# Moving the memory gate into the attention loop, the combination by one step, and two weight splits out of their queue, in an encoder block on one core

## The chip, the cores and the metric

The kernel runs on one core of a Trainium2 chip. A core has a matrix engine (TensorE, PE in the profile; PEld is its loading of weights), a vector engine (VectorE, DVE), an activation engine (ScalarE, ACT), a general engine (GpSimd, POOL) and a queue engine that only starts transfers (SyncE, SP). Each takes its instructions in order. Transfers between the large memory (HBM) and the on-chip memory (SBUF) are DMAs. The accumulators of PE lie in PSUM banks. The metric is device time in microseconds (us) for one execution, less is better.

## The reference

One encoder block on a sequence of 1024 tokens with 1024 channels. Three mixers run on the same normalised input: a windowed attention in three dilation groups (a), a grouped-query attention (b), and an attention into a fixed memory of 256 rows (m). Each is multiplied by a SiLU gate and projected, the three are merged by sigmoid gates, and one output projection follows.

```
h = rms_norm(x, g_pre);  a_qkv, bq, bk, bv, mq, ga, gb, gm, mg = split(h @ w_in)
# a: three groups (window, dilation), combined by the softmax of their log-denominators
wts = softmax(stack(lses));  oa = sum_g wts[g] * outs[g]
# b: rms-normed, axially rotated queries and keys, 8 query heads over 2 key heads
p = softmax(qc . kb * HEAD_DIM ** -0.5);  ob = p @ vb
# m: queries into the memory
pm = softmax(mq . km * M_HEAD_DIM ** -0.5);  om = pm @ vm
ya = (oa * silu(ga)) @ w_br_a;  yb = (ob * silu(gb)) @ w_br_b;  ym = (om * silu(gm)) @ w_br_m
gates = sigmoid(mg + b_merge)
merged = gates[0] * ya + gates[1] * yb + gates[2] * ym
x = x + rms_norm(merged @ w_out, g_post)
```

Everything is float32. The kernel keeps that by splitting an operand into a high and a low part and taking three products (high by high, high by low, low by high).

## The kernel before

The stages follow each other on PE, whose order is written out by hand: projections and the memory attention (to about 200 us), the grouped-query attention (to 461), the products of the windowed attention's values (a Strassen scheme, to 587), the products of its queries and keys (`pair_product`, L1312, 587 to 1079), the windowed attention itself woven with the first 16 of 24 branch units (1079 to 1298), the last 8 units (`y_part`, L2015), and the output projection (L2097). PE is never given work out of this order, so an operand that is late stops it. From the values stage on the order of DVE, ACT, POOL and SP is by hand too.

**Grouped-query attention** (`b_att`). A loop over n does, each for an own lag, `row_max` (n below 128), `scores` ten steps and more later, `pv` and `final`. Between them it yields the time in which another stream of projections is fed to PE. POOL adds up the exponentials of a block (L788), ACT and DVE split the sum (`lh`, `ll`), and `final` multiplies it by a column of ones (L125). `token_block` uses the tiles `tx0`, `tx1`, `tb0` to `tb3` at n = 18 to 90 and not after.

**Third values stage**. 28 steps n (7 products of 4 blocks), each of 12 matmuls (L1273). A dictionary `SIDE` gives for each n the instructions that are issued to the other engines after that step's matmuls: sums (`v3_sum`) on DVE, splits (`v3_split`: high part on ACT, low part on DVE, L105 and L106) of the products' operands S1 to S4, `operand` (the gate of b), `k_load` and the like for the next stage, and, before the change, `memory_operand`: two loads (`od[2, k]` and `g2d[2, k]`) into the two tiles `tab`, 0.5 × a × gate on DVE, a store. The same two tiles are then loaded with a rotation table (`tabA`) which is multiplied by `rb`; the pair products' evacuations read it.

**Windowed attention.** 12 items (4 pairs of heads by 3 groups), each of 8 steps T. `plan` puts the work of a step into a list, `weave` mixes it on PE with the units of `add_y`. After the third group of a pair `combine` gives 12 functions: `fetch` the denominators, `shares`, `weights`, `put` (a store), two loads, two `weigh` (POOL), and so on. `combining(T)` issues the next as long as T equals its entry in `STEP_T`. `tokens(T)` issues what belongs to single items, at the last item the four loads of `rows`, which `shares_3` transposes on PE (L1911).

**Branch units.** Unit m multiplies a column block of the three projections by the gated mixer output. `y_load(m)` loads weights (SP), `y_split(m)` splits them: high part on ACT (L1345), low part on the engine given, DVE or POOL (L1346), into a `wh` tile unless another is given. `th_load` loads the merge gate, and `y_evac` (L1363, L1364) adds the unit up on DVE. Unit m of the weave leaves such calls in the list `pend`, from which the weave takes one at a time. Behind the weave come the rest of `pend`, then `third(1)` (three DVE instructions, L1957 to L1959, the last of the combination of pair 3, which read and free the bank `W3B[2, 1]`), `dl_high(3, hi)` (ACT, L1851), `dl_low`, and the units 16 to 18 in three parts:

```python
for ks in (range(2), range(2, 3)):
    for m in range(16, 19):
        y_part(m, ks)
```

then their fourth blocks of k and the units 19 to 23, each with `y_evac(m - 1)`, at m = 16 and 17 `y_split(m + 3)`.

Of the kernel before, what the change touches and what calls it, by code (L numbers as in the profile page):

```python
# [8 lines left out]
F32 = mybir.dt.float32  # L9
R = mybir.dt.float32r  # L10
AF = mybir.ActivationFunctionType
OP = mybir.AluOpType
# [3 lines left out]
S = 1024  # L16
NT = 8
P = 128
# [32 lines left out]
def block(ctx: ExitStack, tc: tile.TileContext, x, xT, memT, cst, msk, bcst, tabA, gpost,  # L51
          wu, wv, wb, wmem, wbr, wout, out):
    nc = tc.nc
# [120 lines left out]
    pend = []  # L174
# [525 lines left out]
    with tc.tile_pool(name="ba", bufs=1, reuse_waits="tile") as ba:  # L700
# [34 lines left out]
        def token_block(k):  # L735
# [13 lines left out]

            return [sub(0, b12, b11), sub(2, b22, b12), sub(1, b22, T[0]), sub(3, b21, T[1])]  # L750

        def b_att():
            st = {}
            blocks = []
# [66 lines left out]
            for n in range(128 + LAG_F + 8):  # L821
                if n < 128:
                    i, x = divmod(n, 8)
                    row_max(i, x)
                    if n == 1:
                        b_const()
                    if n in (18, 42, 66, 90):
                        blocks += token_block((n - 18) // 24)
                    if blocks and x in (1, 3) and n % 24 != 19:
                        with tc.issue_after(fp["last"].ins):  # L830
                            blocks.pop(0)()
                    yield 216
                    if i % 2 and i < 15 and x == 4:
                        q_prep((i + 1) // 2)
                        yield 436
                else:
                    yield END_PAD
                if n % 8 == LAG_S % 8 and 0 <= n - LAG_S < 128:
                    shift((n - LAG_S) // 8)
                    yield 109  # L840
                m = n - LAG_T
                if m < 0:
                    yield START_PAD + 1000 * (n < 3)
                elif m < 128:
                    scores(*divmod(m, 8))
                    yield 432
                m = n - LAG_P
                if 0 <= m < 128 and m % 8 == 7:
                    pv(m // 8)
                    yield 8 * 432  # L850
                m = n - LAG_F
                if m >= 0 and m % 8 == 7 and m < 128:
                    final(m // 8)
                    yield 432
# [127 lines left out]
    def operand(r, stage):  # L982
# [10 lines left out]
            V.tensor_tensor(ot, ot, rt, op=OP.mult)  # L993
        else:
            nc.sync.dma_start(od[1, k, :, t], OT.pop(r)[0])

    def memory_operand(k, stage):

        if stage == 0:
            nc.sync.dma_start(tab[0], od[2, k])  # L1000
            nc.sync.dma_start(tab[1], g2d[2, k])
        else:
            V.scalar_tensor_tensor(tab[0], tab[0], 0.5, tab[1], op0=OP.mult, op1=OP.mult)
            nc.sync.dma_start(od[2, k], tab[0])

    turn = [0]

# [203 lines left out]
    for n in range(28):  # L1211
# [34 lines left out]
        if k == 3:  # L1246
# [2 lines left out]
    SIDE = {2: [lambda: v3_sum("S2", "A22", "S3", OP.subtract, v3.tile([P, 1024], F32, name="xS2"))],  # L1249
            4: [lambda: v3_split("S2")], 5: [lambda: kt_split("T3", 0)], 6: [lambda: kt_split("T3", 1)],   # L1250
            7: [lambda: operand(7, 1), lambda: operand(7, 2)], 8: [lambda: v3_split("S3")],
            10: [lambda: v3_sum("S4", "A12", "S2", OP.subtract)], 12: [lambda: v3_split("S4")],
            13: [lambda: k_load(0, 0)], 14: [lambda: v3_sum("S1", "A11", "S2", OP.add)], 16: [lambda: v3_split("S1")],
            18: [lambda: k_load(0, 1)], 20: [lambda: v3_split("A22"), lambda: k_load(1, 0)], 22: [lambda: k_load(1, 1)],
            23: [lambda: k_sum(0, 1)], 24: [lambda: k_own(0)], 25: [lambda: [k_sum(0, j) for j in (2, 3)]],
            26: [lambda: k_block(0, "S2")], 27: [lambda: k_block(0, "S1"), lambda: k_block(0, "S3"), lambda: k_sum(0, 4)]}
    for j in range(4):
        for z in range(2):
            SIDE.setdefault(2 + 5 * j + 4 * z, []).append(lambda j=j, z=z: memory_operand(j, z))
    SIDE[22].append(lambda: [nc.sync.dma_start(tab[j], tabA[:, j]) for j in range(2)])  # L1260
    for j in range(2):
        SIDE[26 + j].append(lambda j=j: V.tensor_tensor(tab[1 - j], tab[1 - j], rb, op=OP.mult))
    for n in range(28):
        i, k = divmod(n, 4)
        an, bn = PRODUCTS[i]
# [205 lines left out]
    with ExitStack():  # L1471
# [218 lines left out]
        def plan(it, pre, nxt):  # L1690
# [7 lines left out]
            def tokens(T):  # L1698
# [11 lines left out]
                if n == 11:  # L1710
                    if T == 6:
                        DL["g"] = cb.tile([P, S], F32, name="wgt", bufs=2)
                        nc.sync.dma_start(DL["g"], g2d[0, 3])
                    if T == 5:
                        for j in range(4):
                            nc.scalar.dma_start(rows[16 * j:16 * j + 16],
                                              std[3, j % 2, j // 2].rearrange("s (t a) -> (s t) a", t=NT))

            def ready():
# [104 lines left out]
                    lambda: load(2), load_gate, lambda: weigh(2), gate, store]  # L1824

        todo = []
        STEP_T = (4, 7, 0, 0, 1, 5, 5, 7, 0, 3, 4, 6)
        seq = [(p_, g) for p_ in range(4) for g in range(3)]
        items = [item(*x) for x in seq] + [None]

# [25 lines left out]
        def add_y(m):  # L1856
            n, i, f = steps[m]

            def gen(_):
# [2 lines left out]
                    pend.append(lambda: y_split(m + 1, G))  # L1862
                if m == 15:
                    pend.append(lambda: y_load(18))
                pend.append(lambda: th_load(m + 1))
                for t in half:
                    ps_ = psd()
# [106 lines left out]
        weave(16, every(), FIRST_PAD + 12 * NT * (SOFT + 100.0) + 4 * LAST_PAD + 10500.0)  # L1974
        while pend:
            pend.pop(0)()
        third(1)
        dl_high(3, hi)
        dl_low(3, lo)
        y_split(17)  # L1980
        dl_low(3, hi)
        y_split(18, V, qk.tile([P, S], R, name="aq", bufs=2))
        y_load(19)
        out_pool()
        for nm in ("B11", "B21"):
            for k in range(4):
# [341 lines left out]
```

## Time and profile before

| | us |
|---|---|
| three runs | 1434.96, 1439.09, 1443.1 (median 1439.09) |
| profiled execution | 1439.34, its span 1437.5, mean granted clock 0.988 |
| PE busy | 1395.1 (97%) |
| DVE, ACT, POOL busy | 1023.4, 659.1, 573.1 |

The span is the time between the first and the last instruction that the profile shows; 1.84 us of the execution lie around it. An engine is idle where its next instruction waits for another engine, or for a DMA; the profile names the one that came last. The granted clock is the share of full speed that PE was given in a stretch.

### The profile page before, as it was taken

Reading aid. Unit: us, or ns where it says so; the run is one execution under the profiler, and the core shown is the slowest. Engines: PE = TensorE matmul, PEld = TensorE weight load, DVE = VectorE, ACT = ScalarE, POOL = GpSimd, SP = SyncE. Lnnn points to the kernel's source line nnn. Section 1 sums busy time; section 2 is a strip of 40 time slices with the busy share of each in tenths; the row PEclk is TensorE's granted clock in tenths of the full one; section 3 lists DMA queues with packets and bytes.
Section 4 is the critical chain, followed back from the end, with each engine's and each line's share of the span. In section 5 each row is a group of like instructions: output and inputs, shape, how many; then the busy total and the mean of one; then the engine's idle time right before and its main releaser. Section 6 shows DMA issues by size and latency. Waiting matters only on the chain.

```text
span 1437.5 us, 21813 instructions
## 1 busy us (share of the span) xinstructions
PE 1395.1 (97%) x7775; PEld 1113.6 (77%) x7775; DVE 1023.4 (71%) x1824; ACT 659.1 (46%) x1384; POOL 573.1 (40%) x440
## 2 busy tenths in 40 slices
PE   8999999999999998899999999999999999998997
PEld 7799986666666888788888888888887777776886
DVE  7768578776763786766777776677776556667877
ACT  6544356665645443233333333333346664652332
POOL 1416703767665000244555554455541253360003
PEclk9999999999999999999999999999999999998999
DMA  6356432222111887624332333333365677755455
GB/s 239 96 170 230 167 121 87 97 77 89 63 52 42 284 258 253 208 81 127 102 101 99 108 117 118 103 117 103 118 199 175 211 184 210 226 171 183 141 204 176
DMA packets 120284, 212.29 MB, mean 148 GB/s; under 512 B 32400, under 2 KB 60912, under 8 KB 120176
## 3 DMA queue, kind: packets, MB, share of 16 engines
q1 hardware_dynamic: 110384, 196.88, 42.7%
q10 hardware_dynamic: 9792, 14.03, 2.7%
q8 instruction: 61, 1.00, 0.3%
q14 instruction: 47, 0.39, 0.1%
HBM read 144.48 MB, written 66.38 MB: 147 GB/s over the span
## 4 chain that ended last, share of the span: by engine, by line
PE 52%; DMA 4%; DVE 3%; SPq 1%; POOL 1%; issue 1%; ACT 0%; ACTq 0%; DVEq 0%; POOLq 0%
PE s L1312 33%; PE d L1872 4%; PE s L2097 4%; PE sc L2015 3%; PE s L1572 2%; PE d L2097 2%; PE tr L1644 1%; DMA tab<-g2d 1%; DMA avs<-vdr 1%; PE tr L1611 1%; DMA od<-tab 1%; PE tr L1620 1%; PE tr L1637 1%; DVE acc L1364 0%; DMA tab<-in_tabA 0%
## 5 line engine op out<-in xcount | busy, mean ns | idle before, releaser
L788 POOL TENSOR_TENSOR bl<-bl,bp 128x512 f32<-128x512 f32 x96 | 130.5, 1360 | 54.3 <-ACT bp L784 48.9
L1312 PE MATMUL s<-hh,vS 128*128 128x512 f32 x400 | 133.4, 395 | 0.0
L1312 PE MATMUL s<-vA,vS 128*128 128x512 f32 x450 | 106.6, 390 | 0.0
L106 DVE TENSOR_TENSOR vS<-vot,vS 128x512 fp32r<-128x512 f32 x75 | 86.4, 1152 | 19.9 <-ACT vS L105 19.9
L1585 ACT ACTIVATE pra<-pra,sts 128x192 f32<-128x192 f32 (+2 forms) x176 | 75.4, 430 | 53.2 <-DVE sts L1584 48.7
L1312 PEld LDWEIGHTS s<-vA,vS 128*128 128x128 f32 x450 | 84.5, 188 | 18.3
L784 ACT ACTIVATE bp<-s 128x512 f32<-128x512 f32 x128 | 75.8, 595 | 43.4 <-PE s L782 42.5
L764 DVE TENSOR_REDUCE bn<-tr 128x1 f32<-128x512 f32 x128 | 84.9, 683 | 12.1 <-PE tr L763 11.0
L143 PE MATMUL d<-hh,wh 128*128 128x512 f32 x224 | 89.9, 401 | 2.4 <-DVE fth L216 2.4
L147 PE MATMUL d<-hh,wl 128*128 128x512 f32 x224 | 90.1, 402 | 0.0
L145 PE MATMUL d<-hl,wh 128*128 128x512 f32 x224 | 89.6, 400 | 0.0
L1312 PEld LDWEIGHTS s<-hh,vS 128*128 128x128 f32 x400 | 75.3, 188 | 17.7
L1312 PE MATMUL s<-hh,wl 128*128 128x512 f32 x200 | 79.7, 399 | 2.6 <-DVE wl L106 2.6
L1312 PE MATMUL s<-hh,wh 128*128 128x512 f32 x200 | 79.5, 398 | 0.3 <-ACT wh L105 0.3
L1312 PE MATMUL s<-hl,vS 128*128 128x512 f32 x200 | 79.1, 395 | 0.0
L1312 PE MATMUL s<-hl,wh 128*128 128x512 f32 x200 | 78.7, 394 | 0.0
L1053 POOL TENSOR_TENSOR vot<-wr 128x512 f32<-128x512 f32 x13 | 22.2, 1709 | 127.0 <-DMA vA<-in_wu 127.0
L1623 DVE COPY app<-tr 128x384 f32<-128x384 f32 (+1 forms) x64 | 38.8, 606 | 43.9 <-PE tr L1611 27.6
L1316 ACT ACTIVATE vv<-s 128x512 f32<-128x512 f32 x50 | 29.9, 598 | 85.1 <-PE s L1312 58.6
L797 PE MATMUL ov<-bp,VS 128*64 128x512 f32 x256 | 58.5, 598 | 0.0
L1053 POOL TENSOR_TENSOR vot<-vot,vA 128x512 f32<-128x512 f32 x12 | 19.3, 1609 | 91.5 <-DVE vS L106 91.5
L143 PEld LDWEIGHTS d<-hh,wh 128*128 128x128 f32 x224 | 42.6, 190 | 16.3 <-issue 5.5
(619 smaller groups left out, 4097.6 us busy)
## 6 DMA issues: line engine op xcount, KB each, us to landing
wr<-in_wu SPq DMA_DIRECT2D x40, 512.0 KB
vA<-in_wu SPq DMA_DIRECT2D x24, 512.0 KB
qkd<-ko SPq DMA_DIRECT2D x96, 128.0 KB
wl<-thd SPq DMA_DIRECT2D x24, 512.0 KB
wos<-os SPq DMA_DIRECT2D x12, 512.0 KB
wr<-in_wbr SPq DMA_DIRECT2D x24, 256.0 KB
aq<-qkd SPq DMA_DIRECT2D x12, 512.0 KB
ak<-qkd SPq DMA_DIRECT2D x12, 512.0 KB
```

What stands on the lines that cost most here:

```text
L106: V.tensor_tensor(dst_l, src, dst_h.bitcast(F32), op=OP.subtract)
L143: PE.matmul(dst, wh[:, k, :], hh[k][:, t], start=k == 0, stop=False)
L145: PE.matmul(dst, wh[:, k, :], hl[k][:, t], start=False, stop=False)
L147: PE.matmul(dst, wl[:, k, :], hh[k][:, t], start=False, stop=k == 7)
L764: fp["last"] = V.tensor_reduce(st[i]["n"][:, j, c:c + 1], s, axis=AX.X, op=OP.min)
L784: A.activation(pp, s, AF.Exp, scale=-1.0)
L788: G.tensor_tensor(lsum[i % 2], lsum[i % 2], pp, op=OP.add)
L797: PE.matmul(o[e * 64:e * 64 + 64], VS[:, kt, kv], d.pop(kt), start=kt < 2, stop=kt >= NT - 2)
L1312: PE.matmul(BANK[n, c], a, b, start=k == 0 and q == 0 and not more, stop=k == 3 and q == 2, skip_group_check=c in "XW")
L1585: A.activation(src, src, AF.Exp, scale=-1.0, bias=bias, accum_out=sts[:, h, 1, T:T + 1])
L1872: PE.matmul(ps_, a, b, start=k == 0 and q == 0, stop=k == 3 and q == 2)
L2097: PE.matmul(dst[:, e[0]:e[1]], a, b, start=k == 0 and q == 0, stop=k == 3 and q == 2)
```

## The change

- `memory_operand` leaves the third values stage. In its place `memory_load` and `memory_gate` do the same in `b_att`: the loads at n = 112, 116, 130, 132, in halves of 128 × 512, into the tiles `tx` and `tb`; the gates at n = 128, 129, 137, 139, two DVE instructions and two stores each.
- In `SIDE` the loads of `tabA` move from n = 22 to n = 9, the products by `rb` from n = 26 and 27 to n = 13 and 17.
- `STEP_T` moves most functions of a combination by one step.
- The loads of `rows` go from ACT's queue at T = 5 to SP's, two at T = 2 and two at T = 6.
- `y_split(17)` is left in `pend` at unit 15, with its low part on DVE, into a tile named `ak` (in which the windowed attention keeps its keys). `y_split(18)` (into `aq`, the queries' tile) and `y_load(19)` are issued before `third(1)` instead of at the end.

```diff
@@ -749,6 +749,24 @@
 
             return [sub(0, b12, b11), sub(2, b22, b12), sub(1, b22, T[0]), sub(3, b21, T[1])]
 
+        MT = {}
+
+        def memory_load(k):
+            if k % 2 == 0:
+                t = [ba.tile([P, S], F32, name=f"tx{j}", bufs=1) for j in range(2)]
+                MT[k] = [[x[:, h] for h in half] for x in t]
+            else:
+                t = [ba.tile([P, 512], F32, name=f"tb{j}", bufs=1) for j in range(4)]
+                MT[k] = [t[0:2], t[2:4]]
+            for src, dst in zip((od, g2d), MT[k]):
+                for j in range(2):
+                    nc.sync.dma_start(dst[j], src[2, k, :, half[j]])
+
+        def memory_gate(k):
+            for j, (o, g) in enumerate(zip(*MT.pop(k))):
+                V.scalar_tensor_tensor(o, o, 0.5, g, op0=OP.mult, op1=OP.mult)
+                nc.sync.dma_start(od[2, k, :, half[j]], o)
+
         def b_att():
             st = {}
             blocks = []
@@ -838,6 +856,10 @@
                 if n % 8 == LAG_S % 8 and 0 <= n - LAG_S < 128:
                     shift((n - LAG_S) // 8)
                     yield 109
+                if n in (112, 116, 130, 132):
+                    memory_load((112, 116, 130, 132).index(n))
+                if n in (128, 129, 137, 139):
+                    memory_gate((128, 129, 137, 139).index(n))
                 m = n - LAG_T
                 if m < 0:
                     yield START_PAD + 1000 * (n < 3)
@@ -993,15 +1015,6 @@
             V.tensor_tensor(ot, ot, rt, op=OP.mult)
         else:
             nc.sync.dma_start(od[1, k, :, t], OT.pop(r)[0])
-
-    def memory_operand(k, stage):
-
-        if stage == 0:
-            nc.sync.dma_start(tab[0], od[2, k])
-            nc.sync.dma_start(tab[1], g2d[2, k])
-        else:
-            V.scalar_tensor_tensor(tab[0], tab[0], 0.5, tab[1], op0=OP.mult, op1=OP.mult)
-            nc.sync.dma_start(od[2, k], tab[0])
 
     turn = [0]
 
@@ -1249,17 +1262,14 @@
     SIDE = {2: [lambda: v3_sum("S2", "A22", "S3", OP.subtract, v3.tile([P, 1024], F32, name="xS2"))],
             4: [lambda: v3_split("S2")], 5: [lambda: kt_split("T3", 0)], 6: [lambda: kt_split("T3", 1)], 
             7: [lambda: operand(7, 1), lambda: operand(7, 2)], 8: [lambda: v3_split("S3")],
+            9: [lambda: [nc.sync.dma_start(tab[j], tabA[:, j]) for j in range(2)]],
+            13: [lambda: k_load(0, 0), lambda: V.tensor_tensor(tab[1], tab[1], rb, op=OP.mult)],
+            17: [lambda: V.tensor_tensor(tab[0], tab[0], rb, op=OP.mult)],
             10: [lambda: v3_sum("S4", "A12", "S2", OP.subtract)], 12: [lambda: v3_split("S4")],
-            13: [lambda: k_load(0, 0)], 14: [lambda: v3_sum("S1", "A11", "S2", OP.add)], 16: [lambda: v3_split("S1")],
+            14: [lambda: v3_sum("S1", "A11", "S2", OP.add)], 16: [lambda: v3_split("S1")],
             18: [lambda: k_load(0, 1)], 20: [lambda: v3_split("A22"), lambda: k_load(1, 0)], 22: [lambda: k_load(1, 1)],
             23: [lambda: k_sum(0, 1)], 24: [lambda: k_own(0)], 25: [lambda: [k_sum(0, j) for j in (2, 3)]],
             26: [lambda: k_block(0, "S2")], 27: [lambda: k_block(0, "S1"), lambda: k_block(0, "S3"), lambda: k_sum(0, 4)]}
-    for j in range(4):
-        for z in range(2):
-            SIDE.setdefault(2 + 5 * j + 4 * z, []).append(lambda j=j, z=z: memory_operand(j, z))
-    SIDE[22].append(lambda: [nc.sync.dma_start(tab[j], tabA[:, j]) for j in range(2)])
-    for j in range(2):
-        SIDE[26 + j].append(lambda j=j: V.tensor_tensor(tab[1 - j], tab[1 - j], rb, op=OP.mult))
     for n in range(28):
         i, k = divmod(n, 4)
         an, bn = PRODUCTS[i]
@@ -1711,9 +1721,9 @@
                     if T == 6:
                         DL["g"] = cb.tile([P, S], F32, name="wgt", bufs=2)
                         nc.sync.dma_start(DL["g"], g2d[0, 3])
-                    if T == 5:
-                        for j in range(4):
-                            nc.scalar.dma_start(rows[16 * j:16 * j + 16],
+                    if T in (2, 6):
+                        for j in (0, 1) if T == 2 else (2, 3):
+                            nc.sync.dma_start(rows[16 * j:16 * j + 16],
                                               std[3, j % 2, j // 2].rearrange("s (t a) -> (s t) a", t=NT))
 
             def ready():
@@ -1824,7 +1834,7 @@
                     lambda: load(2), load_gate, lambda: weigh(2), gate, store]
 
         todo = []
-        STEP_T = (4, 7, 0, 0, 1, 5, 5, 7, 0, 3, 4, 6)
+        STEP_T = (4, 0, 1, 1, 2, 6, 6, 7, 2, 3, 4, 6)
         seq = [(p_, g) for p_ in range(4) for g in range(3)]
         items = [item(*x) for x in seq] + [None]
 
@@ -1862,6 +1872,7 @@
                     pend.append(lambda: y_split(m + 1, G))
                 if m == 15:
                     pend.append(lambda: y_load(18))
+                    pend.append(lambda: y_split(17, V, qk.tile([P, S], R, name="ak", bufs=2)))
                 pend.append(lambda: th_load(m + 1))
                 for t in half:
                     ps_ = psd()
@@ -1974,13 +1985,12 @@
         weave(16, every(), FIRST_PAD + 12 * NT * (SOFT + 100.0) + 4 * LAST_PAD + 10500.0)
         while pend:
             pend.pop(0)()
+        y_split(18, V, qk.tile([P, S], R, name="aq", bufs=2))
+        y_load(19)
         third(1)
         dl_high(3, hi)
         dl_low(3, lo)
-        y_split(17)
         dl_low(3, hi)
-        y_split(18, V, qk.tile([P, S], R, name="aq", bufs=2))
-        y_load(19)
         out_pool()
         for nm in ("B11", "B21"):
             for k in range(4):
```

## The prediction

> **What bounds the kernel now.** I read the page's head first, then the waits of TensorE, then stretches of the span with the granted clock, last the chain of what ended last and the instructions around each wait. The head:
>
> ```profile
> span 1437.5 us, 21813 instructions
> PE 1395.1 (97%) x7775; PEld 1113.6 (77%) x7775; DVE 1023.4 (71%) x1824; ACT 659.1 (46%) x1384; POOL 573.1 (40%) x440
> ```
>
> TensorE (PE) is busy for 97% of the span and the diff removes no matmul. So the kernel gets shorter only where PE stands still or runs below full clock. The waits of PE (total, times, longest, in us):
>
> ```profile
> PE s L1273 <- ACT wh L105: 5.8, 1, 5.8
> PE sc L2015 <- ACT wh L1345: 4.5, 1, 4.5
> PE s L1312 <- ACT vv L1316: 2.7, 1, 2.7
> PE s L1312 <- DVE wl L106: 2.6, 1, 2.6
> ...
> PE s L1572 <- DVE sts L1584: 2.0, 3, 1.6
> PE sc L2015 <- DVE acc L1364: 1.9, 1, 1.9
> ```
>
> These six rows, 19.5 us, lie in three places: the third values stage (L1273, and the start of the pair products at L1312), one step of the windowed attention (L1572), and the output units after it (L2015). Each is paid for twice. Two stretches (length; busy us of PE, PEld, DVE, ACT, POOL; granted clock; DMA share; GB/s), each holding one of those short gaps:
>
> ```profile
> 1200.00:1210.00 10.00, 8.45 (x66) 6.68 (x64) 6.27 (x27) 4.56 (x20) 0.00 (x0) 0.83 0.71 214
> 1320.00:1330.00 10.00, 8.13 (x29) 6.23 (x28) 9.90 (x13) 2.71 (x5) 0.00 (x0) 0.83 0.64 220
> ```
>
> If the clock only takes full and half speed, 0.83 over 10 us is 3.4 us at half, which costs PE 1.7 us of work. So a gap of 1.6 or 1.9 us costs about 1.7 us beyond itself.
>
> **A, the third values stage.** The four memory operands (load, gate, store) leave it, and the table's loads and products (`tab`, `rb`) move from its end (n=22, 26, 27) to n=9, 13, 17. The chain (start, us) enters the pair products through the table's load:
>
> ```profile
> 588.39 5.56 DMA tab<-in_tabA
> ...
> 601.42 478.12 PE s L1312 x2076
> ```
>
> The instructions (start, us, engine, operation; in brackets the idle time before and its releaser), and one grouped row (busy us, mean ns):
>
> ```profile
> 556.42 1.23 DVE L1003 SCALAR_TENSOR_TENSOR tab<-tab,tab 128x1024 f32<-128x1024 f32 x1 [7.13 <-DMA tab<-g2d]
> 560.47 1.04 ACT L105 ACTIVATE wh<-vS 128x1024 fp32r<-128x1024 f32 x1
> 538.30 0.28 PE L1273 MATMUL s<-wh,hh 128*128 128x256 f32 x1
> 555.45 0.28 PE L1273 MATMUL s<-wl,ak 128*128 128x256 f32 x1
> 561.56 0.80 PE L1273 MATMUL s<-wh,vA 128*128 128x256 f32 x2 [5.83 <-ACT wh L105]
> L1262 DVE TENSOR_TENSOR tab<-tab,rb 128x1024 f32<-128x1024 f32 x2 | 4.2, 2118 | 0.5 <-DMA tab<-in_tabA 0.5
> ```
>
> The gate of the second operand stands in VectorE's (DVE's) queue ahead of work for the next product; it waits 7.13 us for its load, what is behind it reaches ScalarE (ACT) late, and PE stops for 5.83. At the stage's end the two table products (2.12 each) wait for their load and stand ahead of the evacuations that PE needs: the waits of 2.6 and 2.7. Without waits the stage would be 28 steps of 12 matmuls, 336. The start at 555.45 is the 144th, so one is (555.45 − 538.30)/143 = 0.12, and they take 40.3; then 24 pair-product matmuls, to be taken at 0.23 (the spacing in the rows of part C), are 5.5. That ends at 584.1, where the row stands at 601.42: 17.3 us, gaps and half clock together. What becomes late next is the product's operand S3 itself: what stands behind the gate on DVE moves up, but its own loads are no earlier. I leave 0.8 for that: **16.5**, between 12 (a 2 us wait with its 1.7, and small ones) and 17.3.
>
> **B, the combination a step later.** The fetch of `cpt` stays at T=4; the shares move from T=7 to T=0 of the next item; weights, put, the first two loads and their weighings move one step later, `load_gate` two; the third load and weighing, the gate and the store stay.
>
> ```profile
> 1198.35 0.17 DVE L1783 TENSOR_TENSOR cmn<-cpt 128x16 f32<-128x16 f32 x1 [2.80 <-DMA cpt<-std]
> 1202.85 0.37 PE L1572 MATMUL s<-ak,aq 64*128 64x128 f32 x1 [1.55 <-DVE sts L1584]
> ```
>
> DVE waits 2.80 us for `cpt` in one of the three combinations, and PE then 1.55 for DVE. Those 1.55 and the 1.7 of clock go when the load has one step more: the windowed attention runs from 1079.54 (where the chain's row above ends) to 1298.03 (part C), 12 items of 8 steps, so a step is about 2.2. That is 3.3 at most, 0 if the wait returns; I take **3.0**. Three instructions of 0.2 on DVE, one small one on ACT and the DMAs of `put` and the loads keep their number and lie under PE's matmuls; POOL's weighings, and the splits behind them, are the last rival below. On SP the third load (T=7) now comes one step after the first weighing (T=6), which frees its buffer, instead of two: if that holds SP for a microsecond, it is the loads of the values (`avs`, `avp`) behind it that pay, and these are why I don't take the full 3.3.
>
> **C, the output units.** `y_split(17)` leaves ACT's queue behind `dl_high(3, hi)` and goes into unit 15, in a tile that is free; `y_split(18)` and `y_load(19)` go ahead of `third(1)`.
>
> ```profile
> 1302.07 0.68 DVE L1957 TENSOR_TENSOR og<-tr,og 128x512 f32<-128x512 f32 x1
> 1304.24 0.63 ACT L1851 ACTIVATE hh<-og 128x512 fp32r<-128x512 f32 x1 [2.76 <-DVE og L1959]
> 1304.78 0.61 ACT L1345 ACTIVATE wh<-wr 128x512 fp32r<-128x512 f32 x1
> 1318.81 0.63 ACT L1345 ACTIVATE wh<-wr 128x512 fp32r<-128x512 f32 x1 [5.54 <-PE sc L2015]
> 1298.03 0.40 PE L2015 MATMUL sc<-hh,wh 128*128 128x512 f32 x1
> 1310.37 0.39 PE L2015 MATMUL sc<-hh,aq 128*128 128x512 f32 x1
> 1313.12 0.39 PE L2015 MATMUL sc<-hh,wh 128*128 128x512 f32 x1
> 1323.31 0.52 PE L2015 MATMUL sc<-hh,wh 128*128 128x512 f32 x1 [1.87 <-DVE acc L1364]
> ```
>
> The split of unit 17 starts at 1304.78, right behind `dl_high(3, hi)`, which needs `third(1)` on DVE; PE waits 4.48 for it. Later `y_split(19)` waits 5.54 for a `wh` buffer that units 16 and 17 hold; with `ak` used there is one more. The evacuation of unit 16 stands behind it on DVE, and PE waits 1.87. Units 16 to 18 are 72 matmuls (3 units, 4 blocks of k, 2 halves, 3 products); 12 of them lie between 1310.37 and 1313.12, so one is 0.229 and all are 16.5. From 1298.03 they end at 1314.5 where unit 19 starts at 1323.31. Two splits (0.69 each) now stand ahead of `third(1)` on DVE, whose first instruction (1302.07) frees the banks that unit 18 takes: about 0.6 of wait. So 1323.31 − 1315.1 = 8.2, and the 1.7 of clock after the gap: **9.9**, with 4.5 if half of it returns as a wait for `third(1)`, 10 at most.
>
> **D, the memory gates in the grouped-query attention.** 16 loads, 8 gates of 128x512 and 8 stores come into the last steps of that loop. POOL adds a block there, six at a time; the nearest rows:
>
> ```profile
> 396.37 0.68 DVE L746 TENSOR_TENSOR tb<-tx,tb 128x512 f32<-128x512 f32 x1
> 395.10 1.31 POOL L788 TENSOR_TENSOR bl<-bl,bp 128x512 f32<-128x512 f32 x1
> 396.49 1.72 POOL L788 TENSOR_TENSOR bl<-bl,bp 128x512 f32<-128x512 f32 x1
> 450.58 8.06 POOL L788 TENSOR_TENSOR bl<-bl,bp 128x512 f32<-128x512 f32 x6 [2.25 <-ACT bp L784]
> 459.79 0.39 PE L125 MATMUL tr<-blh,one 128*1 128x512 f32 x1
> ```
>
> An add beside a DVE operation of two SBUF operands takes 1.72 instead of 1.31, 0.41 more. The last block's adds end at 458.64 and PE uses their sum at 459.79, with an ACT operation of some 0.6 between. By the step numbers the first four gates (n=128, 129) come some ten steps before the last sum; if the other four all delay the last sum, it is 1.6, if none, 0. I take **−0.9**; a gain from it is excluded, as it only adds work. [...]
>
> **E, the rows' DMAs.** The four loads of `rows` go from ACT's queue at T=5 to SP's at T=2 and T=6.
>
> ```profile
> 1282.22 0.37 SPq L1713 DMA_DIRECT2D wgt<-g2d  x1
> 1282.82 0.27 PE L1911 MATMUL s<-cs,rows 64*128 64x64 f32 x1
> ```
>
> SP reaches its T=6 work (`wgt<-g2d`) only at 1282.22, and PE transposes `rows` at 1282.82. The last load would be issued near 1283, three issues of about 0.37 on. Its landing is unknown; the wait for the small `cpt` load in part B, 2.80, is the nearest. It would land near 1285.7, so PE waits up to 2.9. If SP gets there earlier, with less to wait for, it is 1 or nothing. I take 1.8, and 1.7 of clock: **−3.5**, between 0 and −5. [...]
>
> **The sum.** 16.5 + 3.0 + 9.9 − 0.9 − 3.5 = 25.0 us. The profiled execution took 1439.34, 1.84 more than its span, and 0.25 above the median of the runs. So 1439.3 − 25.0 = **1414 us**. All terms at their best: 30.6 less, 1409; all at their worst: 9.8 less (12 + 0 + 4.5 − 1.7 − 5), 1429.5.
>
> **Rivals.**
> *The wait in the values stage only moves.* The first table product, at n=13, waits for its load on DVE, ahead of the sum S1 (n=14) and its split (n=16) which PE needs at n=20, 538.30 + 240 × 0.12 = 567.1. Issued at n=9 (551.3) and with 5.56 us on the way, as in the chain, the load is there at 557, behind SP's other work at 562; product, sum and split take some 5 more, 567. The margin is nothing at the late end; 5 us late costs 5 and 3.4 of clock, 8.4: **1422**. For it: SP is in order. Against it: the memory transfers that fill SP's queue and the DMA there are gone. Chance 0.17.
>
> *The output units gain half.* `third(1)` decides all, DVE has no gap from 1302 on, and part C is 5: **1419**. Chance 0.10.
>
> *The diff doesn't do what it says.* `y_split(17)` is popped late from the list of pending work, since that list empties step by step, and runs as before: C is nothing, **1424**. Against it: ACT idles for microseconds before 1304.24 (2.76 at least). Chance 0.06.
>
> *Slower.* POOL's queue is in order. Three combinations put their weighing on it a step later, and behind each stands the split of a unit's weights:
>
> ```profile
> 1211.36 5.79 POOL L1806 TENSOR_TENSOR og<-og,wgt 128x1024 f32<-128x1024 f32 x2 [15.32 <-DMA wgt<-wgd]
> 1219.56 1.30 POOL L1346 TENSOR_TENSOR wh<-wr,wh 128x512 fp32r<-128x512 f32 x1
> 1225.62 0.50 PE L1872 MATMUL d<-bh,wh 128*128 128x512 f32 x1
> ```
>
> The split ends at 1220.9 and PE needs it at 1225.62: 4.7 us of margin, a step eats 2.2, so 2.5 are left. If the weights' loads come L later still, each combination costs L − 2.5 + 1.7. To undo 25 and add 7 it takes L = 11.5 in all three; at 13 it is 36.6 and **1451**. For it: POOL has waited 15.32 for such a load. Against it: it waited with nothing else to do. Chance 0.07.
>
> **How the numbers follow.** The forecast keeps 0.60. A measurement of this kernel can tell 0.5%, 7.2 us, from no change. The forecast, and the first three rivals, are all faster by more than that: 0.93; two of them together with B, D and E at their worst come within 0.5% (1422 + 4.9 + 3.0 + 2.3 = 1432), for which I take 0.05 off, and 0.01 from the slower rival at a small L. So faster 0.88, same 0.06, slower 0.06. The range reaches from 1407, a little below the best of all terms, to 1429, their worst, which takes in the first three rivals too.
>
> **What would show it.** Right: no wait of PE at L1273 above 1.5 us and the pair products' long run starting near 584; clock near 1.0 in the step that was 1200:1210; unit 19 near 25 us earlier; a new wait of PE at L1911 for `rows`. Wrong: a wait of PE on S1's split around n=20, PE waiting on `wh` from POOL behind each weighing, or the span between the pair products' start and the windowed attention no longer the same length.

## The result and the profile after

The changed kernel takes 1425.7 us (median of 6 runs, 1424.16 to 1428.72), the kernel before 1436.5 in the same comparison (1434.29 to 1443.1). The ratio is 0.9923, 95% interval 0.9899 to 0.9946: 0.8% or 11 us less. The forecast was 1414, or 25 us less. The direction and the range held, the size did not: more than half of the expected gain is missing.

The profiled execution of the changed kernel took 1428.24, with a span of 1426.4 us; it lies 2.5 above its median, and the profiled one of the kernel before, 1439.34, lies 2.8 above its own. The span fell by 11.1. Where, the two traces tell by stage: grouped-query attention, third values stage with the pair products, windowed attention, units 16 to 23 (from the first matmul of a stage to the first of the next; length, then busy us of PE, PEld, DVE, ACT, POOL, granted clock, DMA share, GB/s). The kernel before:

```profile
218.98:461.47 242.49, 241.01 (x1042) 153.91 (x1041) 168.71 (x260) 142.97 (x236) 151.05 (x112) 1.00 0.22 72
...
538.30:1079.38 541.08, 529.23 (x2437) 438.74 (x2436) 391.60 (x427) 196.15 (x309) 249.29 (x149) 0.99 0.41 131
1079.38:1298.03 218.65, 213.76 (x2013) 163.35 (x2011) 136.18 (x561) 126.94 (x459) 85.40 (x42) 0.99 0.65 195
1298.03:1352.23 54.20, 47.85 (x193) 38.51 (x192) 40.74 (x53) 16.96 (x30) 0.00 (x0) 0.91 0.52 180
```

The changed kernel:

```profile
219.82:467.59 247.77, 242.93 (x1043) 155.67 (x1041) 175.40 (x268) 142.99 (x236) 151.58 (x112) 0.99 0.28 96
...
544.20:1067.71 523.51, 523.51 (x2438) 435.15 (x2436) 384.01 (x422) 195.70 (x308) 248.65 (x149) 1.00 0.38 123
1067.71:1291.19 223.48, 213.21 (x2013) 162.70 (x2011) 136.58 (x562) 127.28 (x460) 85.44 (x42) 0.98 0.63 191
1291.19:1341.10 49.91, 46.77 (x194) 37.82 (x192) 40.32 (x53) 15.88 (x29) 0.00 (x0) 0.93 0.56 195
```

| stage | before | after | difference | forecast |
|---|---|---|---|---|
| grouped-query attention (D) | 242.49 | 247.77 | +5.3 | +0.9 |
| third values and pair products (A) | 541.08 | 523.51 | −17.6 | −16.5 |
| windowed attention (B, E) | 218.65 | 223.48 | +4.8 | +0.5 |
| units 16 to 23 (C) | 54.20 | 49.91 | −4.3 | −9.9 |
| the rest | 381.1 | 381.7 | +0.6 | 0 |

Part A gave all that was there: in the changed kernel PE is busy for the whole 523.51. Everything else fell short. The waits of PE in the changed kernel (total, times, longest) show what took the place of the old ones:

```profile
PE s L1922 <- DMA rows<-std: 5.1, 1, 5.1
PE tr L781 <- DVE bn L782: 3.8, 2, 3.3
PE sc L2025 <- DVE og L1968: 3.1, 1, 3.1
...
PE tr L1621 <- DVE app L1633: 2.2, 3, 1.3
PE s L1582 <- DVE sts L1594: 1.0, 1, 1.0
```

L1922 is the transpose of `rows` (L1911 before), L781 and L782 the row maxima of the grouped-query attention, L2025 the output units, L1968 the first instruction of `third`, L1621 and L1582 matmuls of the windowed attention. Before, there was no such wait on `rows`, and the row maxima cost 0.7 in all.

### The profile page after: what moved, and what is told of

Same layout as the page of the kernel before. It is cut to its first block, busy times and chain, and to the rows that moved or that the text cites. A ratio compares the mean times of both kernels' runs of the same rounds, so it can differ in the third digit from the quotient of the medians.

```text
span 1426.4 us, 21831 instructions
## 1 busy us (share of the span) xinstructions
PE 1389.7 (97%) x7775; PEld 1110.5 (78%) x7775; DVE 1022.1 (72%) x1828; ACT 658.7 (46%) x1384; POOL 573.1 (40%) x440
## 4 chain that ended last, share of the span: by engine, by line
PE 87%; DVE 5%; ACT 2%; POOL 2%; DMA 2%; issue 2%; ACTq 0%; SPq 0%; DVEq 0%; POOLq 0%
PE s L1322 34%; PE d L1883 5%; PE s L1232 4%; PE s L2107 4%; PE ov L815 4%; PE sc L2025 3%; PE s L1283 3%; PE d L143 3%; PE d L145 3%; PE d L147 3%; PE s L1582 2%; PE tr L1654 2%; PE s L799 2%; PE s L800 2%; PE tr L781 2%
## 5 line engine op out<-in xcount | busy, mean ns | idle before, releaser
L782 DVE TENSOR_REDUCE bn<-tr 128x1 f32<-128x512 f32 x128 | 85.1, 683 | 12.0 <-PE tr L781 10.8
L781 PE MATMUL tr<-KS,QH 128*128 128x512 f32 x128 | 52.2, 407 | 4.7 <-DVE bn L782 3.8
L1356 POOL TENSOR_TENSOR wh<-wr,wh 128x512 fp32r<-128x512 f32 x17 | 21.9, 1289 | 85.6 <-ACT wh L1355 85.6
```

What stands on the lines that cost most here:

```text
L781: PE.matmul(s, QH[:, kv * 4 + j], KS[:, kv, c * 512:c * 512 + 512], start=True, stop=True)
L782: fp["last"] = V.tensor_reduce(st[i]["n"][:, j, c:c + 1], s, axis=AX.X, op=OP.min)
```

## The experiments

Stage lengths below are read from each run's trace as in the table, from one profiled execution of each kernel. Each experiment changes one part of the changed kernel, unless it says more; the ratios are to the kernel before, run in the same comparison.

**E: the rows on ACT again.**

```diff
-                    if T in (2, 6):
-                        for j in (0, 1) if T == 2 else (2, 3):
-                            nc.sync.dma_start(rows...
+                    if T == 5:
+                        for j in range(4):
+                            nc.scalar.dma_start(rows...
```

> The four loads of rows go back to ACT's queue at T=5, all else as in the changed kernel. There PE waits 5.10 us for rows and then runs some 4.6 us at half clock (2.3 us lost). Theory 1 (the small load lands late because three large transfers, wr 256 KB, wl 512 KB and wgt 512 KB, were issued just ahead of it on SP, and 1.25 MB at the 220 GB/s of a busy stretch take 5.8 us): ACT can issue them before wl and wgt, they land some 3.5 us after the issue as before the change, the wait falls below 1.5 us and the windowed attention (223.5 us from its first branch unit to the first output unit) is 5 to 7.4 us shorter, the median near 1419. Rival (the wait is for the data, the statistics stored by the last items, whichever queue loads them): the wait stays at 4 to 5 us and the median at 1425.

Measured: 1421.4 us, ratio 0.9871 (0.9857 to 0.9886). No wait for `rows` is left among PE's, and the windowed attention takes 218.54, 4.9 less: just below the expected 5 to 7.4. The rival (the data are late whichever queue loads them) falls.

**E: the rows on SP, one transfer earlier.** `T == 5` as above, but on `nc.sync`.

> All four loads of rows stay on SP but are issued at T=5, which puts them ahead of the 512 KB of wgt and still behind wr and wl. Theory 1 (a small load lands only after the large ones issued ahead of it): it lands with wl, at about 1273.3 by the times of the changed kernel instead of 1274.7, so PE waits about 3.7 us instead of 5.1. Rival (a load from SP's queue takes 6 us here by itself): it is issued 0.4 us earlier and PE waits 4.7.

Measured: 1422.23, ratio 0.9878 (0.9864 to 0.9893); PE waits 2.60 for `rows`, and the windowed attention takes 220.82. The wait is less than either theory said (3.7 and 4.7). By itself it decides little, since kernels with the unchanged order show waits from 3.2 to 5.1. So the cost was doubled instead.

**E: 512 KB more ahead of the rows.**

```diff
                         nc.sync.dma_start(DL["g"], g2d[0, 3])
+                        nc.sync.dma_start(qk.tile([P, S], R, name="aq", bufs=2).bitcast(F32), g2d[0, 3])
```

> The changed kernel with one more load of 512 KB issued on SP between wgt and the last two loads of rows. In five profiles with the changed order PE waited 5.1, 4.0, 3.2, 4.2 and 3.9 us for rows, 4.1 in the mean. Theory 1 (rows land behind the bytes issued ahead of them; 512 KB at 220 GB/s take 2.4 us): 6.5 us, between 5.5 and 7.5. Rival (latency of SP's small loads, whatever is ahead): 4.5, the one issue of 0.4 more.

The additional load goes into a tile that nothing reads. SP in the changed kernel, and PE's wait:

```profile
1266.66 0.57 SPq L1350 DMA_DIRECT2D wr<-in_wbr  x1
1267.33 0.38 SPq L1363 DMA_DIRECT2D wl<-thd  x1
1267.80 0.38 SPq L1723 DMA_DIRECT2D wgt<-g2d  x1
1268.23 0.88 SPq L1726 DMA_DIRECT2D rows<-std  x2
...
1274.81 0.34 PE L1922 MATMUL s<-cs,rows 64*128 64x64 f32 x1 [5.10 <-DMA rows<-std]
```

With the additional load:

```profile
1276.04 0.34 PE L1923 MATMUL s<-cs,rows 64*128 64x64 f32 x1 [6.59 <-DMA rows<-std]
```

The wait is 6.6, as expected from the bytes (6.5), where latency alone gave 4.5, and the windowed attention takes 226.14. In the changed kernel SP does issue the last two loads about when the forecast said, from 1268.23 to 1269.11; PE is ready for them at 1269.71. They are 8 KB each, but 1.25 MB were issued just ahead of them, and PE has them only 5.7 us after SP has issued the last.

The DMA packets recorded in the traces show the same directly. The two loads are 32 packets of 512 bytes; in the changed kernel these start from 1271.77 to 1273.95, when 196 to all 256 of the packets of `wl` and `wgt` are done, and with the additional load from 1272.95 to 1275.20, when 287 to all 384 are. The whole kernel takes 1425.06, ratio 0.9912 (0.9888 to 0.9936), which is not clear of the changed kernel's 0.9923; its profiled execution, 1429.11, is the slowest of the four (the others 1424.16 to 1425.56). In the run on ACT, which has no wait for `rows`, the last load of `rows` is issued ahead of the large ones (queue of ACT, then of SP):

```profile
1268.36 0.34 ACTq L1726 DMA_DIRECT2D rows<-std  x1
```

```profile
1268.94 0.57 SPq L1350 DMA_DIRECT2D wr<-in_wbr  x1
1269.61 0.38 SPq L1363 DMA_DIRECT2D wl<-thd  x1
1270.08 0.38 SPq L1723 DMA_DIRECT2D wgt<-g2d  x1
```

That the position among the transfers matters is shown on SP's queue alone: 2.60 us of wait with one large load fewer ahead, 3.2 to 5.1 as changed, 6.6 with one more. Whether ACT's queue also helps as such was not tried by itself and stays open.

**D: the gates behind the last row maximum.**

```diff
             for j, (o, g) in enumerate(zip(*MT.pop(k))):
-                V.scalar_tensor_tensor(o, o, 0.5, g, op0=OP.mult, op1=OP.mult)
+                with tc.issue_after(fp["last"].ins):
+                    V.scalar_tensor_tensor(o, o, 0.5, g, op0=OP.mult, op1=OP.mult)
```

> The eight memory gates are held behind the last row maximum on DVE (n=127), where the step numbers of the diff seem to put them; in the changed kernel the trace has them between the 111th and the 119th of 128. Theory 1 (the 3.27 us wait of PE in the row maxima, and the 6.8 us at half clock behind it, come from three gates in a row ahead of a row maximum, stretched by POOL's adds): that wait and the clock loss are gone, the grouped-query attention is 4.5 to 5.5 us shorter than the 247.8 of the changed kernel, less what the gates cost at the end. What I predicted for that place, 0.9 us for the last block's sum (0 to 1.6), is then seen too: between 242.5 (its length before the change) and 244. Rival (the loads and stores cost it, not the gates' place): the length stays above 246.

(`issue_after` holds an instruction behind another one on its engine; `fp["last"]` is the row maximum issued last.) First what happens in the changed kernel. DVE:

```profile
409.22 1.62 DVE L767 SCALAR_TENSOR_TENSOR tx<-tx,tx 128x512 f32<-128x512 f32 x1
410.77 0.68 DVE L767 SCALAR_TENSOR_TENSOR tx<-tx,tx 128x512 f32<-128x512 f32 x1
412.08 1.03 DVE L767 SCALAR_TENSOR_TENSOR tb<-tb,tb 128x512 f32<-128x512 f32 x1
```

POOL and PE there:

```profile
409.02 1.28 POOL L806 TENSOR_TENSOR bl<-bl,bp 128x512 f32<-128x512 f32 x1 [1.11 <-ACT bp L802]
411.04 1.52 POOL L806 TENSOR_TENSOR bl<-bl,bp 128x512 f32<-128x512 f32 x1 [0.75 <-ACT bp L802]
...
413.77 0.79 PE L781 MATMUL tr<-KS,QH 128*128 128x512 f32 x1 [3.27 <-DVE bn L782]
```

The diff writes the gates behind n = 128, but the order of DVE in this stage is not the program's: it is arranged when the kernel is built. Four gates come after 110 of the 128 row maxima, four after 118. Three of them stand in a row, but for one instruction, directly ahead of the 111th maximum. The gate at 410.77, which starts between two of POOL's adds, takes 0.68; the two that start beside a running add take 1.62 and 1.03. The maximum comes 3.3 late, PE waits 3.27.

The other four gates stand in a row too, from 424.07 to 427.64, and no wait of PE is seen there: it has the 16 matmuls of `pv` and projections to do, without a gap from 422.47 to 427.79. So a row of gates cost PE time here only where PE came back to DVE before the row was through.

In the run with the gates behind the last maximum that wait is gone, but the stage takes 249.1, more than before, and theory 1's expected 242.5 to 244 falls. The gates now stand ahead of the last shift:

```profile
439.89 0.68 DVE L768 SCALAR_TENSOR_TENSOR tb<-tb,tb 128x512 f32<-128x512 f32 x1
440.49 1.78 DVE L768 SCALAR_TENSOR_TENSOR tx<-tx,tx 128x512 f32<-128x512 f32 x1
442.20 1.75 DVE L768 SCALAR_TENSOR_TENSOR tb<-tb,tb 128x512 f32<-128x512 f32 x1
443.97 0.69 DVE L791 TENSOR_TENSOR QL<-tr,cs 4x512 fp32r<-4x512 f32 x1
...
444.72 0.80 PE L801 MATMUL s<-QL,KB 68*128 68x512 f32 x1 [2.52 <-DVE QL L791]
```

Total 1426.65, ratio 0.9911 (0.9895 to 0.9928). The rival's "above 246" came true, but not for its reason: no DMA releases a wait of PE there.

**D: the gates behind the last shift, and spread.** The first pins them to the shift (`fp["shift"]`), at n = 131, 132, 139, 141. The second puts one gate behind each of the maxima of n = 119, 121, 123, 125, the other four behind the last shift.

> The memory gates are held behind the last shift on DVE (block 15's QL), with the loads of the last two operands at n = 133 and 134. With the gates behind the last row maximum (the run before) four gates of 0.8 to 1.8 us stood ahead of that QL, PE waited 2.52 us for it and ran 6.8 us at half clock, and the attention took 249.1 us. Theory 2 (it is the order on DVE that costs: whatever stands behind a group of gates is late by the group's length, and PE waits if it is a row maximum or a shift): neither wait appears and the grouped-query attention takes 242.5 to 244 us, which is also the 0 to 1.6 that I had put on the last block's sum. Rival (the 16 loads and 8 stores slow what shares the DMA engines and SP's queue): 246 or more, with PE waiting for something that a DMA releases.

> The first four gates are spread over the row maxima, one behind each of n = 119, 121, 123 and 125, the other four behind the last shift. Theory 2 (a single gate, even stretched to 1.8 us by POOL, fits into the slack between two row maxima, three in a row don't): no wait of PE above 0.5 us there, 242.5 to 244 us. If DVE has no slack at all in the loop, each gate delays PE by its length, in all 4 to 7 us, and the attention takes 246 to 250.

Measured: 244.74 and 1423.86 us, ratio 0.9902 (0.9878 to 0.9925), for the first, 0.7 above the expected 242.5 to 244; 243.85 and 1422.1, ratio 0.9887 (0.9861 to 0.9914), for the second, inside it. By the whole kernel's time neither is clear of the changed kernel, as the intervals overlap; it is the stage that tells them apart. Neither old wait appears. The first has a new one, the very one that the forecast had in mind, the last block's sum held up on POOL:

```profile
452.10 9.39 POOL L807 TENSOR_TENSOR bl<-bl,bp 128x512 f32<-128x512 f32 x6 [1.95 <-ACT bp L803]
```

```profile
462.21 0.40 PE L125 MATMUL tr<-blh,one 128*1 128x512 f32 x1 [1.00 <-ACT blh L105]
```

Six adds take 9.39 instead of 8.06, and PE waits 1.00. With the gates spread no wait of PE in this stage is above 0.5, so here single gates fit between two maxima.

**D left out.** Loads, gates and stores of the memory operand are not issued.

> The changed kernel without loads, gates and stores of the memory operand: it leaves out the gating of the memory attention's result. It measures part D whole. Theory 2 (the gates cost only by where they stand on DVE): the grouped-query attention takes 242.3 to 242.7 us as before the change, against 247.8 in the changed kernel, 249.1 behind the last row maximum, 244.7 behind the last shift and 243.9 spread; so 5.3 for the change's placing and 1.4 for the best one. Rival (the start of the stage, the bank order or the clock shifted it in any case): 244 or more also here.

Measured: the attention takes 242.78, 0.1 above the expected band; the whole kernel 1419.28, ratio 0.9869 (0.9844 to 0.9894). So the part costs 5.0 as the change places it, and 1.1 spread. These lengths repeat: with the change's own placing the stage takes 246.8 to 248.0 in six profiles, behind the last shift 244.7 and 244.8 in two, spread 243.9 to 244.1 in three.

**C: `third(1)` ahead of the leftovers.**

```diff
+        third(1)
         while pend:
             pend.pop(0)()
         y_split(18, V, qk.tile([P, S], R, name="aq", bufs=2))
         y_load(19)
-        third(1)
```

> third(1) is issued ahead of the calls left over in pend (on DVE two evacuations of unit 15, four instructions, 2.7 us) and of the split of unit 18 (0.6 us). Theory 1 (the 3.14 us wait of PE ahead of unit 17 is for the PSUM bank that the first instruction of third(1) frees, which stands behind these on DVE): the wait goes from 3.14 to below 0.3, the half clock behind it goes with it, and the units 16 to 23 take 44 to 45.5 us instead of 49.9; the median is 4 to 6 us below 1425.7. Rival (unit 17 waits for its weights or for the accumulators): the wait stays near 3, or moves to unit 18's weights, and the units stay above 48 us.

In the changed kernel, DVE and PE:

```profile
1295.83 0.68 DVE L1356 TENSOR_TENSOR aq<-wr,aq 128x512 fp32r<-128x512 f32 x1
1296.43 0.69 DVE L1968 TENSOR_TENSOR og<-tr,og 128x512 f32<-128x512 f32 x1
```

```profile
1297.26 0.76 PE L2025 MATMUL sc<-hh,ak 128*128 128x512 f32 x1 [3.14 <-DVE og L1968]
```

Unit 17 has its weights (`ak`) and waits for the bank that `third(1)` reads. In the experiment:

```profile
1293.11 0.47 PE L2025 MATMUL sc<-hh,ak 128*128 128x512 f32 x1 [1.21 <-DVE og L1968]
```

The wait falls from 3.14 to 1.21, not below 0.3: one more evacuation is taken from `pend` before `third(1)`. The units take 45.45, the kernel 1422.07, ratio 0.9878 (0.9863 to 0.9892): 3.6 below 1425.7, where 4 to 6 were expected. The rivals (weights, accumulators) fall.

**B: the old steps.** On the kernel with the rows on ACT, `STEP_T` as before the change.

> The loads of rows on ACT as in the run that undid that part, and STEP_T as before the change: only the combination's step is undone against that run. There the windowed attention took 218.54 us, and 218.65 before the whole change. My prediction's part B says that the later step saves 3.0 (0 to 3.3): the windowed attention would take 221.5 here, with a wait of PE near 1.5 us behind DVE's wait for cpt and 3.4 us at half clock. Theory 2 (the waits have only changed places: with the new step PE waits 1.28, 0.98 and 0.62 us, 2.9 together, where DVE does the shares and the weights at the start of an item): within 0.7 of 218.5, and those three waits are gone.

Measured: the windowed attention takes 216.54, against 218.54 with the changed steps; 1419.58, ratio 0.9873 (0.985 to 0.9896). The forecast's 221.5 falls, and theory 2's band, within 0.7 of 218.5, is missed too, by 1.3. The ratios of the two whole kernels, 0.9871 and 0.9873, do not differ. The wait of 1.5 is back, and those of 1.28, 0.98 and 0.62 are gone. Where the first of them comes from, POOL and DVE in the changed kernel show:

```profile
1140.28 1.27 POOL L1356 TENSOR_TENSOR wh<-wr,wh 128x512 fp32r<-128x512 f32 x1 [5.32 <-ACT wh L1355]
```

```profile
1140.47 1.14 DVE L1802 TENSOR_TENSOR cdn<-ceg,cpt 128x48 f32<-128x48 f32 x1
...
1143.03 0.55 DVE L1633 COPY app<-tr 128x384 f32<-128x384 f32 x1
```

```profile
1143.73 0.30 PE L1621 MATMUL tr<-cs,pra 128*128 128x128 f32 x1 [1.29 <-DVE app L1633]
```

The weights stand ahead of the copy that PE waits for, and the first of them, which starts beside a split on POOL, takes 1.14 instead of 0.20.

**All mended, twice.** First the rows on ACT, the gates behind the last shift, and `third(1)` issued with `third(0)`:

> Three edits of the changed kernel together: rows' loads on ACT at T=5, the gates behind the last shift, and third(1) issued with third(0), ahead of all of unit 15's evacuations on DVE (in the run with third(1) ahead of pend, one evacuation still stood before it and 1.21 us of wait were left). By the stages: grouped-query attention 243 (248 in the changed kernel), windowed attention 218.5 (223.5), units 16 to 23 44.2 (49.9): 15.7 us less than the changed kernel, a median near 1411 and 1.8 to 2% below the kernel before. If the gains don't add up, because the output units then wait for the weights or the accumulators of unit 15, the last is 47 and the median 1414.

Measured: 1414.33, ratio 0.9834 (0.9812 to 0.9856), where 1411 was expected, and 1414 if the gains did not add up. The attention takes 244.8 instead of 243, and the units 45.42 instead of 44.2, as PE now waits 1.17 for unit 18's split. So this split went ahead of the leftovers and the gates were spread, once with the old steps and once with the changed ones:

> Of the change, the tables and the memory operand out of the third values stage, the split of unit 17 in its new place, and the gates spread (four among the row maxima, four behind the last shift); the loads of rows on ACT and STEP_T as before the change; third(1) with third(0), then the split of unit 18, then the evacuations left of unit 15 (in the best run so far PE waited 1.17 us for that split, which stood behind them). By stages: grouped-query attention 243.9, windowed attention 216 to 217, units 16 to 23 44.3 to 45: a median of 1410 to 1412, 1.7 to 2.0% below the kernel before.

> The kernel beside it in this call with the changed STEP_T: a direct measurement of the combination's step. My prediction's part B (3.0 saved by the later step) gives 3 us less than its neighbour; theory 2 (the later step trades one wait of 1.5 us for three of 2.9 together) gives 0.8 to 2 us more, all of it in the windowed attention, and by how much depends on whether the clock drops behind the 1.5 us wait.

Old steps: 1412.4, ratio 0.982 (0.98 to 0.9841). Changed steps: 1413.21, ratio 0.9823 (0.9804 to 0.9842). Both beat the changed kernel by about 1%, and the kernel before by 1.8%. Units 16 to 23 take 44.1, the attention 244.0 and 244.1, the windowed attention 218.08 (expected 216 to 217) and 217.07. The changed steps are 0.8 slower in the median, at the low end of theory 2's 0.8 to 2, but the windowed attention, where all of it was expected, is 1.0 shorter with them. The waits of PE with the old steps:

```profile
PE s L369 <- ACT hh L270: 6.5, 1, 6.5
PE d L143 <- DVE fth L216: 2.4, 1, 2.4
PE s L1584 <- DVE sts L1596: 2.0, 3, 1.6
```

Of the large ones only the one of B is left, besides two near the start that no part touches. So B is worth nothing that these runs can tell. With the rows on ACT the windowed attention took 218.54, 217.34 and 217.07 with the changed steps, 216.54 and 218.08 with the old ones, and the two medians differ by less than the spread of their runs. Why the same steps give 216.5 once and 218.1 once is the next point.

**The clock behind a gap.** Three kernels with the same 3.14 us wait ahead of unit 17, each 10 us from about there. The changed kernel:

```profile
1294.00:1304.00 10.00, 6.86 (x19) 5.34 (x19) 9.37 (x15) 4.19 (x8) 0.00 (x0) 0.66 0.88 315
```

The rows on ACT:

```profile
1288.00:1298.00 10.00, 6.86 (x23) 5.36 (x23) 9.46 (x15) 4.29 (x9) 0.00 (x0) 0.83 0.92 318
```

The rows on SP at T=5:

```profile
1290.00:1300.00 10.00, 6.95 (x31) 5.79 (x32) 9.16 (x15) 3.99 (x8) 0.00 (x0) 1.00 0.87 322
```

The clock records of the traces of the kernel before and of the changed kernel have only full and half speed (in the changed kernel 0.50 from 412.10 to 418.93, 1272.26 to 1279.09 and 1296.15 to 1302.98, and 1.00 between these), so by 0.66, 0.83 and 1.00 the three pieces of 10 us hold 6.8, 3.4 and 0 us at half clock. And the wait of 1.5 to 1.6 that the old steps leave, in the mended kernel with the old steps and in the run of part B:

```profile
1185.00:1195.00 10.00, 8.39 (x71) 6.94 (x71) 5.23 (x22) 4.58 (x18) 0.00 (x0) 0.83 0.72 190
```

```profile
1187.00:1197.00 10.00, 8.48 (x79) 6.51 (x78) 6.05 (x24) 4.58 (x18) 0.68 (x1) 1.00 0.74 197
```

Nearly the same wait, 1.61 and 1.52, is followed by 3.4 us at half clock in the first and by none in the second.

The traces show where such gaps differ. In each of them the stretches at half clock begin and end on one grid of 3.41 us: in the changed kernel they begin at 53.70, 412.10, 1272.26 and 1296.15, the last three 105, 357 and 364 times 3.4133 behind the first, which lasts 3.41 where they last 6.83. On that grid the 3.14 us gap lies as 2.04 and 1.10 in two intervals in the changed kernel (6.8 at half clock), as 0.39 and 2.75 with the rows on ACT (3.4), as 1.42 and 1.72 with the rows on SP (none). The gap of 1.61 lies in one interval, that of 1.52 as 0.24 and 1.27 in two. Between 60 and 1395 us in the fourteen traces, every interval at full clock with 1.87 us or more of idle PE was followed by half clock (24 intervals; 1.87, 2.56 and 2.04 in the changed kernel, 3.28, 1.87, 2.15 and 1.87 in the kernel before), none with less than 1.5; between them it was 2 of 7 (one with 1.55 in the kernel before).

## Why the prediction was right and wrong

- **A was right in mechanism and size**: 17.6 where the sum had 16.5, between 12 and 17.3. The 0.8 left for waits was not needed. The rival that the wait only moves to S1 found nothing: no wait of PE is left in that stage. No run undoes A alone; the account rests on the waits of the trace, and on 523.5 to 523.8 us for these stages in all thirteen traces that have this part.
- **B failed at "lie under PE's matmuls".** The forecast took 3.0 for a wait of 1.55 that goes, with its clock. The wait goes, and three others of 2.9 together come; the largest, 1.29, because the weights now stand on DVE ahead of the copy that PE waits for. Net: from 2.0 lost (216.54 to 218.54, of which 1.1 is a wait of PE for ACT that only that profile has) to 1.0 gained (218.08 to 217.07). The old steps' 218.08 holds 3.4 us at half clock, an estimated 1.7 of it lost; without that it would be 216.4. So, by this estimate, the later step loses some 0.5 to 1 unless the 1.5 us gap that it removes lies in one interval of that grid. (A step is 218.49/96 = 2.28, not 2.2, which changes nothing here.)
- **C failed at "frees the banks that unit 18 takes".** It is unit 17 that takes the bank, 12 matmuls or 2.7 us earlier. So the wait for the weights (4.48) gave way to one for the bank (3.14), 4.3 us instead of 9.9; in the mean of nine profiles with this tail (48.5 us) 5.7. The rival "the output units gain half" had the mechanism, `third(1)`, and the price, 5.
- **D failed at "by the step numbers".** The forecast placed the gates where the diff writes them and charged only POOL's stretching there, 0.9. They ran among the row maxima and cost 5.3 with the clock (5.0 against the kernel without them). But the place was not all: behind the last row maximum, about where the forecast had them, they cost 6.3 (249.1 against 242.78). By the diff's own step numbers the last shift, at n = 130, stands behind the four gates of n = 128 and 129 on DVE, and PE waited 2.52 for it. What the gates delay on DVE itself, a row maximum or the shift, is the term that the forecast put at nothing. The row chosen, a POOL add of 1.72 instead of 1.31, was also only one side: DVE's own operation was stretched from 0.68 to as much as 1.78. In the changed kernel the gate of 409.22 ends at 410.84, 0.5 after the POOL add that runs to 410.30.
- **E was right in sign and kind**, and its landing was mis-sized. A small load's 2.80 was carried over from another place, where some 0.7 MB (`wl`, `avs` and two of `avp`, issued in the 2.2 us before it) stood ahead of it and not 1.25. The wait was 5.1 instead of 1.8 (3.2 to 5.1, 4.0 in the mean, in six profiles with this order). These six give 222.7 for the windowed attention in the mean, the three with the rows on ACT and the changed steps 217.7: 5.0, the far end of the forecast's 0 to 5, where it took 3.5.
- **The sum.** The misses against the forecast are +1.1 (A), −4.3 (B and E together), −5.6 (C), −4.4 (D), −0.6 (the rest): together −13.8, which but for rounding is the 11.1 measured less the 25.0 forecast. C and D failed by the most, then B: with E at 4.9 (223.48 less 218.54), 1.4 worse than forecast, B is left with 0.1 instead of 3.0. The slower rival (POOL's weighing) did not occur in the changed kernel: no wait of PE on POOL's part of a split is among its larger ones. Two other profiles with the changed steps (the rows on SP at T=5, and `third(1)` ahead) show one such wait of 1.0.
- **What stays open**: whether ACT's queue helps the loads of `rows` by itself, and whether B is worth a microsecond either way. That the rest is 0.6 longer says nothing: the grouped-query attention starts at 219.82 instead of 218.98, and at 218.2 to 219.9 in the thirteen traces that have the same work ahead of it.

## What to carry to other kernels

Work that is moved out of a crowded stage is paid where it lands: read who waits for that engine there, instruction by instruction, and make sure where the order on the engine is really set. Ask of each instruction that the moved work comes ahead of how soon the bottleneck engine needs it. Loads of 8 KB reached PE here 5.7 us after the last of them was issued, with 1.25 MB issued just ahead, so move a small transfer by its position among the large ones and not by its own size. When a wait for one operand goes, look up what else that same matmul needs (here a bank) before booking the whole wait.

## What the runs showed of the hardware

An operation of DVE with two SBUF operands, 0.68 us alone, took up to 1.78 beside a POOL add, one of 0.20 took 1.14 beside a POOL split, and an add took 1.52 instead of 1.28. Loads of 8 KB issued behind 1.25 MB of others held PE for 3.2 to 5.1 us, behind 1.75 MB for 6.6. And the same gap of PE of 3.14 us was followed by 0, 3.4 or 6.8 us at half clock in different runs, one of 1.5 to 1.6 by 0 or 3.4: the stretches at half clock lay on a grid of 3.41 us, and how the gap of 3.14 lay on it differed from run to run (2.04 and 1.10, 0.39 and 2.75, 1.42 and 1.72 us in two neighbouring intervals), so a forecast should carry the clock's price of a gap as a range.
